# Order edges between weight splits, a later fourth token sum and another tile for two weight pairs, in a float32 decoder layer on one core

## The chip, the cores and the metric

The kernel runs on one core of one Trainium2 chip. The metric is device time in microseconds (us) of one execution, the median over the runs. The core has five engines with a queue each, which they work off in order: TensorE (PE), VectorE (DVE), ScalarE (ACT), GpSimd (POOL) and SyncE (SP), which here only issues DMAs. An engine waits for another one, or for a DMA, by semaphores; what stands behind a waiting instruction on its queue waits with it.

## The reference

One decoder layer with D = 1024, 1024 tokens and a hidden width of 4096, all float32:

```python
z = h @ w_in                       # pool group | q | k | v
y_pool = pool_mixer(u_pool, w_pool, pool_scale)
y_attn = sliding_window_attention(q, k, v, attn_sinks)   # window 128, ALiBi, sinks
mix = concatenate([y_pool, y_attn]) @ w_out
h = layer_norm(DEEPNORM_ALPHA * h + mix, ln1_g, ln1_b)
ff = square(relu(h @ w_ff1)) @ w_ff2
h = layer_norm(DEEPNORM_ALPHA * h + ff, ln2_g, ln2_b)
h = h + sigmoid(h @ w_ple_gate + b_ple_gate) * (p @ w_ple)
```

## The kernel before, in words

**Split products.** A float32 operand is split into a high part, a cast to the reduced type fp32r on ACT (`high`, L98), and a low part, source minus high on DVE (`low`, L103). A product of two split operands is three matmuls (`mm3`): high by high (L112), high by low (L113), low by high (L114). A "product" of the feed-forward layer (`prod`) is four such triples, 12 matmuls of 128x128 by 128x512. It reads one split weight part (tag "ws", six buffers) and one split token matrix in `X` (tag "c", six buffers, or "x7").

**Stages.** First come z, attention and pooling; then the output projection in a left and a right half of columns, for token blocks 0 to 3 and then 4 to 7. `out_left(t, ...)` loads eight weight blocks in four pairs, splits each pair into a "w" tile, of which there are two buffers, and multiplies each by four token blocks; `residual` (L431) adds the sum to the token rows. Layer norm and transposes follow (`norm1`), whose results for blocks 4 to 7 are also combined into the token matrices T1, T2 and T3: with a and b the two transposed halves, T1 = a - (first half of the tokens), T2 = b - T1, T3 = b - a. T4 is made out of T2 by two more adds with X["21"] and a split (`last_sum(c)`, c the token block): three operations on DVE and one on ACT for each of four blocks. While norm1 runs, products a11 and a12 of the first eight weight pairs (NPRE = 8) are made by `early`.

**The first feed-forward matrix.** The main loop (L719 to L735) works a Strassen-Winograd form: a pair p of weight blocks needs the products a11, a12, s2, s3, s1, s4 and a22, seven for p of 8 and above and the last five for p below 8. `source` loads the pair's weights into a "w" tile (four blocks, 1 MB, two buffers) and makes sums of them on DVE: s2 by two adds into a "st" tile, s3 by one add in place, s4 by one more. The order of products is p0: s2, s3, s1, s4; p1: s2, s3, s1, s4; a22 of p0; a22 of p1; then pair after pair. T2 goes with s2, T3 with s3, T1 with s1 and s4 with X["22"]; T4 goes with a22. The loop makes each weight split AHEAD = 4 turns before the product that uses it; in its first four turns it makes only splits, and the T4 sum of one token block each. `finish` adds the products up on DVE and squares the hidden blocks, on ACT mostly; POOL stores them.

**What sets the order.** The source is traced in program order, and the tile framework's scheduler orders each engine's instructions by its own timing model, within the dependences. What the program can add is an edge: instructions traced inside `with tc.issue_after(ins)` stay behind `ins` on its engine. Before, the loop has none.

**After the loop**: the second feed-forward matrix (to about 828 us), the second norm, the gate and the embedding product.

Of the kernel before, what the change touches and what calls it, by code (L numbers as in the profile page):

```python
# [8 lines left out]
F32R = mybir.dt.float32r  # L9
# [3 lines left out]
P = 128  # L13
D = 1024
S = 1024
HALF = 512
# [47 lines left out]
AHEAD = 4  # L64
# [3 lines left out]
def layer(ctx, tc, xT, x, pT, w_in, w_pool, pscale, sinks, w_out, ln1, w1, w2, ln2, w_ple, w_gate, bgate, bias, rcount, out):  # L68
    nc = tc.nc
# [6 lines left out]
    def nm(s):  # L76
        uid[0] += 1
        return f"{s}_{uid[0]}"
# [4 lines left out]
    def wt(shape, dt=F32R):  # L83
        return sb.tile(shape, dt, tag="w", bufs=2, name=nm("w"))

    def nat(shape, dt=F32):
        return sb.tile(shape, dt, tag="n", bufs=8, name=nm("n"))
# [8 lines left out]
    def high(dst, src, scale=None):  # L96
        if scale is None:
            nc.scalar.copy(out=dst, in_=src)  # L98
        else:
            nc.scalar.mul(out=dst, in_=src, mul=scale)  # L100

    def low(eng, dst, src, hi):
        return eng.tensor_tensor(out=dst, in0=src, in1=hi.bitcast(F32), op=ALU.subtract)  # L103
# [60 lines left out]
    def acc_ps():  # L164
        return ps.tile([P, HALF], F32, tag="mm", bufs=3, name=nm("mm"))
# [224 lines left out]
    def layer_norm(y, gb, root=False):  # L390
        st = small([P, 2, 6])
        for i in range(2):
            nc.vector.bn_stats(out=st[:, i, :], in_=y[:, i * HALF : (i + 1) * HALF])
        mv = small([P, 8])
        nc.vector.bn_aggr(out=mv[:, 0:2], in_=st.rearrange("p a b -> p (a b)"))
        v, r0, e, r, m = (mv[:, i : i + 1] for i in range(2, 7))
        nc.vector.tensor_scalar(out=v, in0=mv[:, 1:2], scalar1=LN_EPS, scalar2=None, op0=ALU.add)
        if root:
            nc.vector.reciprocal(out=r0, in_=v)
            nc.scalar.activation(out=r0, in_=r0, func=AF.Sqrt)  # L400
        else:
            nc.gpsimd.tensor_tensor(out=r0, in0=v, in1=mhalf, op=ALU.pow)

        nc.vector.scalar_tensor_tensor(out=e, in0=r0, scalar=v, in1=r0, op0=ALU.mult, op1=ALU.mult)
        nc.vector.tensor_scalar(out=e, in0=e, scalar1=-0.5, scalar2=1.5, op0=ALU.mult, op1=ALU.add)
        nc.vector.tensor_tensor(out=r, in0=r0, in1=e, op=ALU.mult)
        nc.vector.tensor_scalar(out=m, in0=mv[:, 0:1], scalar1=-1.0, scalar2=None, op0=ALU.mult)
        nc.scalar.activation(out=y, in_=y, func=AF.Identity, bias=m, scale=1.0)
        nc.vector.scalar_tensor_tensor(out=y, in0=y, scalar=r, in1=gb[0], op0=ALU.mult, op1=ALU.mult)
        add(y, y, gb[1])  # L410
# [4 lines left out]
    def transposed(y, j, pt):  # L415
        for k in range(4):
            kt = 4 * j + k
            nc.tensor.transpose(pt[:, k, :], y[:, kt * P : (kt + 1) * P], ident)  # L418
        return pt

    def out_load(dst, dh, kk, st, eng):
        load_split(dst[:, 0], dst[:, 1], w_out[dh, kk], None, eng, st)

    def out_mm(o, n, k, w):
        m = (mixP if k < 4 else mixA)[n // 4]
        c = (n % 4) * P
        mm3(o, m[:, 0, k % 4, c : c + P], m[:, 1, k % 4, c : c + P], w[:, 0, k % 2, :], w[:, 1, k % 2, :], k == 0, k == NK - 1)
# [3 lines left out]
        nc.vector.scalar_tensor_tensor(out=v, in0=v, scalar=ALPHA, in1=o, op0=ALU.mult, op1=ALU.add)  # L431


    def out_left(t, staging, eng):
        blocks = range(4 * t, 4 * t + 4)
        os = [acc_ps() for _ in range(3)]
        os.append(ps.tile([P, HALF], F32, tag="s", bufs=2, name=nm("s")))
        for k in range(NK):
            if k % 2 == 0:
                w = wt([P, 2, 2, HALF])  # L440
                out_load(w, 0, k // 2, staging(), eng)
            for n in blocks:
                out_mm(os[n % 4], n, k, w)
        return os
# [51 lines left out]
    def wide(tag, shape, dt):  # L496
        return p1.tile(shape, dt, tag=tag, bufs=1, name=nm(tag))


    X = {}  # L500
# [4 lines left out]
    def split_to(name, c, src, eng):  # L505
        cs = slice(c * P, (c + 1) * P)
        dh = X[name][:, 0, :, cs]
        high(dh, src)
        low(eng, X[name][:, 1, :, cs], src, dh)

    def norm1(n):
        t, c = n // 4, n % 4
        layer_norm(hn[n], gb1)
        a = transposed(hn[n], 0, tr_ps())
        b = transposed(hn[n], 1, tr_av())
        nc.scalar.mul(out=hn[n], in_=hn[n], mul=ALPHA)
        nc.scalar.dma_start(out=h_dram[n], in_=hn[n])
        if t == 0:
            if c < 3:
                nc.scalar.copy(out=pre[:, 4 + c].rearrange("p (k t) -> p k t", k=4), in_=a)  # L520
            split_to("11", c, a, nc.vector)
            split_to("21", c, b, nc.vector)
        else:
            r12, t1, t2 = temp((P, 4, P)), temp((P, 4, P)), nat([P, 4, P])
            nc.scalar.copy(out=r12, in_=a)
            if c < 3:
                add(t1, a, pre[:, 4 + c].rearrange("p (k t) -> p k t", k=4), ALU.subtract)
            else:
                for i in range(2):
                    add(t1, t1 if i else a, block("11", i, c), ALU.subtract)  # L530
            add(t2, b, t1, ALU.subtract)
            split_to("22", c, b, nc.vector)
            add(r12, b, r12, ALU.subtract)
            split_to("T1", c, t1, nc.vector)
            split_to("T2", c, t2, nc.vector)
            split_to("T3", c, r12, nc.vector)
            diff[c] = t2


    diff = {}  # L540

    def last_sum(c):
        t2 = diff[c]
        for i in range(2):
            add(t2, block("21", i, c), t2, ALU.add if i else ALU.subtract)
        split_to("T4", c, t2, nc.vector)

    def w_split(src):
        s = part()
        high(s[:, 0], src)  # L550
        low(nc.vector, s[:, 1], src, s[:, 0])
        return s

    def prod(o, s, name, more=False):
# [27 lines left out]
    for j in range(2):  # L582
        w = big([P, 2, 2, 2, HALF])
# [7 lines left out]
        out_right(n)  # L591
    X["11"], X["21"] = (big([P, 2, 4, HALF]) for _ in range(2))
    pre = wide("pre", [P, NPRE, HALF], F32)
    os = out_left(1, lambda: nat([P, 2, HALF]), nc.vector)
    residual_load(1)
    for n in range(4):
        norm1(n)
# [22 lines left out]
    def source(p, name):  # L620
        first = p >= NLAST and name in ("a11", "a12")
        if (p, first) not in raws:
            r = raws[p, first] = wt([P, 2 if first else 4, 4, P], F32)
            nc.sync.dma_start(out=r, in_=w1[p, :, 0:2] if first else w1[p])
        r = raws[p, first]
        if name in BLOCK:
            return r[:, BLOCK[name]]
        if name == "s2":
            sums[p] = stage([P, 2, 4, P])
            add(sums[p][:, 0], r[:, 2], r[:, 3])  # L630
            add(sums[p][:, 1], sums[p][:, 0], r[:, 0], ALU.subtract)
        elif name == "s3":
            add(r[:, 2], r[:, 0], r[:, 2], ALU.subtract)
            return r[:, 2]
        elif name == "s4":
            add(sums[p][:, 1], r[:, 1], sums[p][:, 1], ALU.subtract)
        return sums[p][:, 0 if name == "s1" else 1]
# [29 lines left out]
    def finish(p, name):  # L667
        if name == "a11":
            U[p, 1] = temp()
            nc.scalar.copy(out=U[p, 1], in_=B[p, "A"])  # L670
        elif name == "s2":
            U[p, 2] = temp()
            add(U[p, 2], pre[:, p] if p < NPRE else U[p, 1], B[p, "B"])
        elif name == "s3":
            U[p, 3] = temp()
            add(U[p, 3], U[p, 2], B[p, "Y"])
        elif name == "s1":
            hidden_block(p, 1, 1, square_sum(U[p, 3], B[p, "Z"]))
        elif name == "a12":
            hidden_block(p, 0, 0, lambda dst: relu2(dst, B[p, "A"]))  # L680
        elif name == "a22":
            hidden_block(p, 1, 0, square_sum(U[p, 2], B[p, "Y"]))
        else:
            hidden_block(p, 0, 1, square_sum_v(U[p, 2], B[p, "Z"]))
# [4 lines left out]
    order = []  # L689
# [26 lines left out]
                nc.sync.dma_start(out=second, in_=src)  # L716
                blocks[u].append(second)

    ready, lows = {}, []  # L719
    for i in range(len(order) + AHEAD):  # L720
        if i == order.index((NLAST, "a11")):
            begin = wide("pre", [P, 4, 2, HALF], F32)
            for u in range(4):
                fetch(u)
        if i < len(order):
            ready[i] = w_split(source(*order[i]))
        if i < AHEAD:
            last_sum(i)
            continue
        p, name = order[i - AHEAD]  # L730
        xb, where, more = STEPS[name]
        if not more:
            B[p, where] = bank()
        prod(B[p, where], ready.pop(i - AHEAD), xb, more)
        finish(p, name)  # L735


    hidden = {}
# [80 lines left out]
    for u, (i, q) in enumerate(units):  # L819
        k = QORDER.index(q)  # L820
# [129 lines left out]
```

## Time and profile before

| | us |
| --- | --- |
| runs | 1013.18, 1011.62, 1015.57; median 1013.18 |
| the profiled execution's own time | 1010.05 |
| its span on the engines | 1008.1 |
| PE busy | 989.4 (98%) |
| DVE, ACT, POOL busy | 704.4, 457.2, 129.1 |

A timeline row gives start, duration, engine, source line, operation with output and inputs, count, and in square brackets how long the engine had been idle and what ended that. Names are the program's tags; "mm", "f" and "s" are accumulators in PSUM, "pt" and "av" transposes in PSUM, "c" and "x" split token matrices, "ws" a split weight part, "w" a weight tile, "st" a staging tile, "n" and "t" token or hidden blocks. Durations overlap at their ends: 128x512 matmuls in a row start 0.227 us apart though each is listed with 0.39. A row of the waits view gives the engine, what it was about to do, what it waited for, and us in total, times and the longest in us. The loop's first product stands at 315.82, and the second matrix begins at about 575.

### The profile page before, as it was taken

How to read it: one execution, taken by the hardware profiler on the slowest of the kernel's cores; microseconds unless marked ns; L12 is line 12 of the kernel's file. 1: busy time of each engine (PE TensorE's matmuls, PEld its weight loads, DVE VectorE, ACT ScalarE, POOL GpSimd, SP SyncE). 2: the span in 40 equal slices, each digit the busy share in tenths (PEclk: the TensorE clock that was granted, in tenths of full speed). 3: DMA queues.
4: the chain of work that ended last, by engine and by line, in shares of the span. 5: the costliest groups of instructions: out<-in, count | busy, mean ns of one | idle time of the engine just before them, and what ended most of it. 6: DMA issues, size and time to landing. Idle time of an engine off the chain costs nothing.

```text
span 1008.1 us, 12163 instructions
## 1 busy us (share of the span) xinstructions
PE 989.4 (98%) x4556; PEld 820.5 (81%) x4556; DVE 704.4 (70%) x1119; ACT 457.2 (45%) x735; POOL 129.1 (13%) x158
## 2 busy tenths in 40 slices
PE   8999999999999999899999999999999999999998
PEld 7877887887887888788888888888888888888887
DVE  5789679566888757655456666787647699997333
ACT  5667567524475433343444343433433354651111
POOL 0034265620000000100000000100011110000000
PEclk9999999999999999999999999999999999999999
DMA  6511423324152533664174793776798874621011
GB/s 214 179 62 46 164 63 126 125 84 146 64 189 105 188 96 106 225 179 146 63 249 168 278 320 132 167 239 200 209 211 186 202 174 125 202 81 42 37 38 42
DMA packets 38715, 148.00 MB, mean 147 GB/s; under 512 B 4736, under 2 KB 5632, under 8 KB 35840
## 3 DMA queue, kind: packets, MB, share of 16 engines
q1 hardware_dynamic: 29664, 116.29, 34.3%
q0 software_dynamic: 7840, 26.74, 11.3%
q10 hardware_dynamic: 1152, 4.19, 1.0%
q8 instruction: 35, 0.57, 0.2%
q14 instruction: 24, 0.20, 0.1%
HBM read 124.66 MB, written 22.54 MB: 146 GB/s over the span
## 4 chain that ended last, share of the span: by engine, by line
PE 59%; DVE 2%; DMA 1%; ACT 0%; issue 0%; DVEq 0%; ACTq 0%
PE f L114 19%; PE f L113 19%; PE f L112 19%; DMA w<-in_w 1%; PE f L418 1%; DVE ws L103 1%; DVE st L117 0%; DVE n L117 0%; DVE t L117 0%; DVE w L117 0%; ACT ws L98 0%; DVE n L663 0%; DVE t L892 0%; DVE t L890 0%; DVE t L893 0%; ACT t L891 0%
## 5 line engine op out<-in xcount | busy, mean ns | idle before, releaser
L114 PE MATMUL f<-c,ws 128*128 128x512 f32 (+1 forms) x456 | 174.6, 386 | 3.2 <-DVE ws L103 3.2
L112 PE MATMUL f<-c,ws 128*128 128x512 f32 (+1 forms) x456 | 175.3, 386 | 1.5 <-ACT c L98 1.5
L113 PE MATMUL f<-c,ws 128*128 128x512 f32 (+1 forms) x456 | 175.7, 385 | 0.0
L113 PE MATMUL f<-x,w 128*128 128x512 f32 x448 | 174.3, 389 | 0.0
L114 PE MATMUL f<-x,w 128*128 128x512 f32 x448 | 174.3, 389 | 0.0
L112 PE MATMUL f<-x,w 128*128 128x512 f32 x448 | 147.1, 389 | 0.0
L98 ACT CAST w<-st 128x1024 fp32r<-128x1024 f32 (+2 forms) x67 | 67.0, 999 | 111.6 <-issue 68.7
L103 DVE TENSOR_TENSOR w<-st,w 128x1024 fp32r<-128x1024 f32 (+2 forms) x63 | 74.2, 1180 | 49.5 <-ACT w L98 49.2
L114 PEld LDWEIGHTS f<-c,ws 128*128 128x128 f32 x456 | 85.7, 188 | 20.9 <-DVE ws L103 3.8
L112 PEld LDWEIGHTS f<-c,ws 128*128 128x128 f32 x456 | 85.6, 188 | 19.0 <-ACT c L98 1.9
L113 PEld LDWEIGHTS f<-c,ws 128*128 128x128 f32 x456 | 85.7, 188 | 17.1
L114 PEld LDWEIGHTS f<-x,w 128*128 128x128 f32 x448 | 84.1, 188 | 17.6
L113 PEld LDWEIGHTS f<-x,w 128*128 128x128 f32 x448 | 84.0, 188 | 17.5
L112 PEld LDWEIGHTS f<-x,w 128*128 128x128 f32 x448 | 84.1, 188 | 17.3
L103 DVE TENSOR_TENSOR x<-ws,x 128x1024 fp32r<-128x1024 f32 x52 | 63.3, 1218 | 0.0
L112 PE MATMUL mm<-c,w 128*128 128x512 f32 x152 | 60.8, 405 | 1.9 <-ACT w L98 1.2
L98 ACT CAST ws<-w 128x512 fp32r<-128x512 f32 x60 | 37.1, 622 | 52.3 <-PE f L114 42.7
L114 PE MATMUL mm<-c,w 128*128 128x512 f32 x152 | 60.4, 401 | 0.0
L113 PE MATMUL mm<-c,w 128*128 128x512 f32 x152 | 60.2, 397 | 0.0
L98 ACT CAST ws<-st 128x512 fp32r<-128x512 f32 x48 | 29.7, 620 | 62.5 <-PE f L114 52.9
L98 ACT CAST x<-ws 128x1024 fp32r<-128x1024 f32 x52 | 54.5, 1049 | 0.0
L117 DVE TENSOR_TENSOR n<-t,f 128x512 f32<-128x512 f32 x48 | 32.0, 682 | 31.4 <-PE f L114 31.4
(200 smaller groups left out, 1815.9 us busy)
## 6 DMA issues: line engine op xcount, KB each, us to landing
ws<-in_w SPq DMA_DIRECT2D x70, 512.0 KB, 4.1
w<-in_w SPq DMA_DIRECT2D x16, 1024.0 KB, 5.3
c<-fd SPq DMA_DIRECT2D x6, 2048.0 KB, 9.0
fd<-n POOLq DMA_DIRECT2D x20, 512.0 KB, 4.1
ws<-in_w POOLq DMA_DIRECT2D x20, 512.0 KB, 7.0
st<-in_w_in SPq DMA_DIRECT2D x18, 512.0 KB, 3.5
w<-in_w SPq DMA_DIRECT2D x10, 512.0 KB, 4.2
n<-in_x SPq DMA_DIRECT2D x8, 512.0 KB, 5.0
```

The lines of the kernel that those rows point to most:

```text
L98: nc.scalar.copy(out=dst, in_=src)
L103: return eng.tensor_tensor(out=dst, in0=src, in1=hi.bitcast(F32), op=ALU.subtract)
L112: nc.tensor.matmul(o, ah, bh, start=first, stop=False, skip_group_check=more)
L113: nc.tensor.matmul(o, ah, bl, start=False, stop=False, skip_group_check=more)
L114: nc.tensor.matmul(o, al, bh, start=False, stop=last, skip_group_check=more)
L117: nc.vector.tensor_tensor(out=o, in0=a, in1=b, op=op)
L418: nc.tensor.transpose(pt[:, k, :], y[:, kt * P : (kt + 1) * P], ident)
```

## The change

Three edits, with no instruction added or removed.

1. In the second `out_left` (blocks 4 to 7) the pairs for k = 4 and k = 6 are split into one tile with the tag "x7" of its own instead of the third and fourth "w" tile. That tag's buffer is later used by X["22"].
2. `w_split` records its low instruction in `lows`, and every weight split of the loop, with the sums that `source` makes for it, is traced behind an edge from the low before it. The first split of the fifth turn has its edge from the low of T3 for the last token block instead. All edges are on DVE, the engine of `low`.
3. `last_sum(c)` moves from the first four turns of the loop to behind the first four products, and behind an edge from the low of T3 for the last token block. For this `split_to` returns its low, and `diff[c]` keeps it.

```diff
-    def out_left(t, staging, eng):
+    def out_left(t, staging, eng, room=None):
...
-                w = wt([P, 2, 2, HALF])
+                w = room[:, k // 2 - 2] if room is not None and k > 3 else wt([P, 2, 2, HALF])
...
-        low(eng, X[name][:, 1, :, cs], src, dh)
+        return low(eng, X[name][:, 1, :, cs], src, dh)
...
-            split_to("T3", c, r12, nc.vector)
-            diff[c] = t2
+            diff[c] = t2, split_to("T3", c, r12, nc.vector)
...
-        t2 = diff[c]
+        t2 = diff[c][0]
...
+    lows = []
+
     def w_split(src):
         s = part()
         high(s[:, 0], src)
-        low(nc.vector, s[:, 1], src, s[:, 0])
+        lows.append(low(nc.vector, s[:, 1], src, s[:, 0]))
         return s
...
-    os = out_left(1, lambda: nat([P, 2, HALF]), nc.vector)
+    os = out_left(1, lambda: nat([P, 2, HALF]), nc.vector, wide("x7", [P, 2, 2, 2, HALF], F32R))
...
-    ready, lows = {}, []
+    ready = {}
     for i in range(len(order) + AHEAD):
...
         if i < len(order):
-            ready[i] = w_split(source(*order[i]))
+            with tc.issue_after((diff[3][1] if i == AHEAD else lows[-1]).ins):
+                ready[i] = w_split(source(*order[i]))
         if i < AHEAD:
-            last_sum(i)
             continue
...
         finish(p, name)
+        if i - AHEAD < 4:
+            with tc.issue_after(diff[3][1].ins):
+                last_sum(i - AHEAD)
```

The scheduler makes the following of it. Names below carry buffer numbers, which are mostly one lower after the change.

DVE in the second `out_left`, before: the lows of the two last weight pairs (w_346, w_348) stand behind a layer norm's last operations (L409, L117).

```order
L405 TENSOR_SCALAR sm_367_2325<-sm_367_2325 128x1
L406 TENSOR_TENSOR sm_367_2325<-sm_367_2325 128x1
L409 SCALAR_TENSOR_TENSOR n_310_1846<-n_310_1846,sm_367_2325,st_329_1990 128x1024
L117 TENSOR_TENSOR n_310_1846<-n_310_1846,st_330_1991 128x1024
L103 TENSOR_TENSOR w_346_2163<-n_347_2164,w_346_2163 128x1024
L103 TENSOR_TENSOR w_348_2192<-n_349_2193,w_348_2192 128x1024
```

After:

```order
L103 TENSOR_TENSOR w_345_2135<-n_346_2136,w_345_2135 128x1024
L316 TENSOR_TENSOR y_286_1733<-av_301_1810,yl_306_1831 64x512
L103 TENSOR_TENSOR x7_338_2101<-n_347_2164,x7_338_2101 128x1024
L103 TENSOR_TENSOR x7_338_2101<-n_348_2192,x7_338_2101 128x1024
L431 SCALAR_TENSOR_TENSOR n_307_1840<-n_307_1840,mm_331_1994 128x512
L103 TENSOR_TENSOR ws_379_2466<-ws_378_2464,ws_379_2466 128x512
```

The two lows (now into x7_338) stand ahead of the first residual add (L431) of the right half for blocks 0 to 3, 47 rows earlier.

DVE at the loop's start, before. c_375 is T1, c_376 T2, c_377 T3 and c_378 T4, t_438 T3's sum, st_454 and w_453 the second pair's weights.

```order
L117 TENSOR_TENSOR st_454_2975<-st_454_2975,w_453_2973 128x512
L117 TENSOR_TENSOR w_453_2973<-w_453_2973 128x512
L103 TENSOR_TENSOR c_378_2464<-n_423_2749,c_378_2464 128x4x128
L117 TENSOR_TENSOR n_440_2866<-av_437_2857,t_439_2865 128x512
L103 TENSOR_TENSOR ws_452_2966<-st_448_2940,ws_452_2966 128x512
L103 TENSOR_TENSOR c_375_2461<-t_439_2865,c_375_2461 128x4x128
L103 TENSOR_TENSOR ws_455_2978<-st_454_2975,ws_455_2978 128x512
L103 TENSOR_TENSOR x7_374_2460<-av_437_2857,x7_374_2460 128x4x128
L117 TENSOR_TENSOR t_438_2864<-av_437_2857,t_438_2864 128x512
L117 TENSOR_TENSOR st_454_2975<-w_453_2973,st_454_2975 128x512
L103 TENSOR_TENSOR c_376_2462<-n_440_2866,c_376_2462 128x4x128
L103 TENSOR_TENSOR ws_458_2997<-w_453_2973,ws_458_2997 128x512
```

After, where c_374 to c_377 are T1 to T4, t_437 T3's sum, and st_453 and w_452 the second pair's weights:

```order
L117 TENSOR_TENSOR n_439_2865<-av_436_2856,t_438_2864 128x512
L103 TENSOR_TENSOR ws_451_2953<-st_447_2939,ws_451_2953 128x512
L103 TENSOR_TENSOR c_374_2460<-t_438_2864,c_374_2460 128x4x128
L103 TENSOR_TENSOR x7_373_2459<-av_436_2856,x7_373_2459 128x4x128
L117 TENSOR_TENSOR t_437_2863<-av_436_2856,t_437_2863 128x512
L103 TENSOR_TENSOR c_375_2461<-n_439_2865,c_375_2461 128x4x128
L103 TENSOR_TENSOR c_376_2462<-t_437_2863,c_376_2462 128x4x128
L117 TENSOR_TENSOR st_453_2958<-w_452_2956 128x512
L117 TENSOR_TENSOR n_388_2514<-c_336_2099,n_388_2514 128x512
L117 TENSOR_TENSOR n_405_2631<-c_336_2099,n_405_2631 128x512
L117 TENSOR_TENSOR n_422_2748<-c_336_2099,n_422_2748 128x512
L117 TENSOR_TENSOR n_439_2865<-c_336_2099,n_439_2865 128x512
```

The lows of T2 and T3 now come ahead of everything of the second pair and of the T4 sums (n_388 to n_439). The T4 sums of all four blocks, eight adds and then four lows, stand in one stretch among the splits of the second pair. On PE the loop now begins with the whole of one product after another (s2 with T2, s3 with T3, s1 with T1); before, it did one matmul of s2 and one of s3, then the whole of s1, and then the rest.

DVE between pairs 7 and 8, before. st_538 and w_537 belong to pair 7, st_556 and w_552 to pair 8.

```order
L117 TENSOR_TENSOR t_536_3589<-pre_337_2100,f_535_3576 128x512
L103 TENSOR_TENSOR ws_534_3573<-w_525_3491,ws_534_3573 128x512
L117 TENSOR_TENSOR st_556_3711<-w_552_3691 128x512
L117 TENSOR_TENSOR st_556_3711<-st_556_3711,w_552_3691 128x512
L117 TENSOR_TENSOR w_552_3691<-w_552_3691 128x512
L117 TENSOR_TENSOR n_519_3450<-t_524_3489,f_531_3518 128x512
L117 TENSOR_TENSOR n_521_3469<-t_524_3489,f_528_3499 128x512
L103 TENSOR_TENSOR ws_539_3596<-st_538_3593,ws_539_3596 128x512
```

After, with st_537 and w_536 of pair 7 and st_555 and w_551 of pair 8:

```order
L103 TENSOR_TENSOR ws_546_3653<-st_537_3592,ws_546_3653 128x512
L103 TENSOR_TENSOR ws_548_3672<-w_536_3590,ws_548_3672 128x512
L117 TENSOR_TENSOR n_545_3649<-t_535_3588,f_542_3617 128x512
L117 TENSOR_TENSOR n_547_3668<-t_535_3588,f_539_3598 128x512
L117 TENSOR_TENSOR t_550_3688<-pre_337_2100,f_549_3675 128x512
L103 TENSOR_TENSOR ws_552_3692<-w_551_3690,ws_552_3692 128x512
L117 TENSOR_TENSOR st_555_3710<-w_551_3690 128x512
L664 SCALAR_TENSOR_TENSOR n_545_3649<-n_545_3649 128x512
```

Pair 8's adds stood ahead of the low of pair 7's first product (ws_539); they now stand behind all five lows of pair 7 (the last is ws_548), and its first split (ws_552) is of a raw block.

On SP two loads of token rows (L449) are now issued one ahead of and one behind the second `early` weight load (L566), where both stood behind it, and four loads for the second matrix (L708) stand together behind a load of pair weights instead of two on each side of it. From about 575 us on, the order is as before.

## The prediction

> **What bounds the kernel now.** I read the page's busy times first, then the windows by stage, then what TensorE waited for. The page:
>
> ```profile
> span 1008.1 us, 12163 instructions
> PE 989.4 (98%) x4556; PEld 820.5 (81%) x4556; DVE 704.4 (70%) x1119; ACT 457.2 (45%) x735; POOL 129.1 (13%) x158
> ```
>
> TensorE (PE) is busy 98% of the span. The change takes no matmul away, so it can gain only PE's idle time. The windows (us of the window, then busy time and count of PE, weight loads, DVE, ACT and POOL; PE's granted clock; DMA share; GB/s) say where that lies:
>
> ```profile
> 200.00:317.70 117.70, 114.58 (x536) 94.31 (x534) 92.43 (x170) 61.12 (x99) 12.83 (x17) 1.00 0.36 126
> 317.70:412.20 94.50, 91.31 (x402) 75.15 (x402) 60.62 (x98) 34.11 (x57) 4.29 (x8) 1.00 0.34 121
> 412.20:575.00 162.80, 162.80 (x718) 134.85 (x719) 95.35 (x148) 71.01 (x121) 10.49 (x17) 1.00 0.53 182
> 575.00:828.00 253.00, 253.00 (x1117) 209.46 (x1117) 183.90 (x192) 101.27 (x107) 22.67 (x26) 1.00 0.76 209
> 828.00:1003.50 175.50, 175.48 (x835) 147.05 (x834) 118.54 (x175) 57.41 (x73) 3.11 (x4) 1.00 0.25 84
> ```
>
> From 412.2 to 1003.5 PE has no gap to give. Before 200 the change alters nothing. What is left is 117.70 - 114.58 = 3.12 and 94.50 - 91.31 = 3.19 us. PE's waits name them:
>
> ```profile
> PE f L114 <- DVE ws L103: 3.2, 1, 3.2
> ...
> PE f L112 <- ACT c L98: 1.5, 1, 1.5
> PE mm L113 <- DVE w L103: 1.4, 1, 1.4
> ...
> PE mm L112 <- DVE n L431: 0.2, 1, 0.2
> ```
>
> Three of the four stand where the change works. A gap costs a little more than the wait, since the matmul after it is followed later than the usual 0.227 us; I count from start to start.
>
> **The change part by part.** The instructions stay the same in number and shape, but for order and buffers.
>
> *Weight pairs in another tile.* In the second half of the output projection PE stops here:
>
> ```profile
> 230.49 0.60 PE L418 MATMUL pt<-ident,n 128*128 128x128 f32 x4
> ...
> 232.62 0.27 PE L418 MATMUL pt<-ident,n 128*128 128x128 f32 x1
> 234.32 0.50 PE L113 MATMUL mm<-w,c 128*128 128x512 f32 x1 [1.44 <-DVE w L103]
> 225.45 0.39 PE L113 MATMUL mm<-w,c 128*128 128x512 f32 x1
> 226.04 0.50 PE L112 MATMUL mm<-w,c 128*128 128x512 f32 x1 [0.20 <-DVE n L431]
> ```
>
> From 232.62 to 234.32 is 1.70 us, of which I leave 0.2 to the transpose itself: the gap is worth 1.5 us. It waits for the low half of a weight pair, which VectorE (DVE) makes at 233.05 because ScalarE (ACT) casts the pair only at 230.38, when a "w" buffer is free:
>
> ```profile
> 230.38 1.98 ACT L98 CAST w<-n 128x1024 fp32r<-128x1024 f32 x2
> 233.05 2.35 DVE L103 TENSOR_TENSOR w<-n,w 128x1024 fp32r<-128x1024 f32 x2
> 210.56 2.33 ACT L98 CAST ws<-ws 128x512 fp32r<-128x512 f32 x4 [7.40 <-DMA ws<-in_w]
> 205.25 0.69 DVE L431 SCALAR_TENSOR_TENSOR n<-n,mm 128x512 f32<-128x512 f32 x1 [2.75 <-PE mm L114]
> 211.22 1.29 DVE L103 TENSOR_TENSOR ws<-ws,ws 128x512 fp32r<-128x512 f32 x2 [4.55 <-ACT ws L98]
> ```
>
> The new tile is free from the start, and the raw pairs have long been loaded. The two casts (1.98) and the two subtractions (2.35) move to about 203 to 207, where ACT idles 7.40 us and DVE 2.75 and 4.55. The residual add at 205.25 slips by about 1.4 us; behind it only norm statistics are queued, before that idle 4.55. PE needs the pair near 230.5, so 23 us cover it: **-1.5 us**. Without that cover the price is at most the old gap. The raw pairs' buffers come free earlier, so one token load passes one weight load on SyncE's (SP) queue; that weight's sums feed products after 255, which leaves room. The other gap in these rows, 226.04 - 225.45 - 0.23 = 0.36 us, waits for a residual add that stays where it is: 0 to -0.36, and I take 0.
>
> *Fourth token sums behind the first products.* At the loop's start PE does one matmul of the T2 product and then waits for T3's last cast:
>
> ```profile
> 315.82 0.39 PE L112 MATMUL f<-c,ws 128*128 128x512 f32 x1
> 317.69 0.73 PE L112 MATMUL f<-c,ws 128*128 128x512 f32 x2 [1.49 <-ACT c L98]
> 317.02 0.62 ACT L98 CAST c<-t 128x512 fp32r<-128x512 f32 x1
> 315.65 0.68 DVE L117 TENSOR_TENSOR t<-av,t 128x512 f32<-128x512 f32 x1
> 316.85 0.69 DVE L103 TENSOR_TENSOR c<-n,c 128x512 fp32r<-128x512 f32 x1
> 318.05 0.69 DVE L103 TENSOR_TENSOR c<-t,c 128x512 fp32r<-128x512 f32 x1
> 323.92 0.69 DVE L117 TENSOR_TENSOR t<-pre,f 128x512 f32<-128x512 f32 x1 [1.60 <-PE f L114]
> ```
>
> T3's sum is made at 315.65 because sums for T4, and three adds on the next pair's weights, stand ahead on DVE. DVE issues one such operation every 0.60 us (316.85 to 318.05 is 1.20 for two). Now nine of the twelve T4 operations that stood ahead of this point, and the three adds, go behind T3. With 0.60 each from the last PSUM transpose I get T2's last low ready at 313.2 and T3's at 314.0; PE arrives, 1.5 earlier than before, at 314.3 and needs T2's low at 314.5 and T3 at 317.1, a whole T2 product (2.72) later. The gap, 317.69 - 315.82 - 0.23 + 0.11, is **-1.75 us**.
>
> What is late next: twelve T4 operations, 12 x 0.60 = 7.2 us on DVE, now stand among the splits of the second pair's weights. By the same count the low half for its T3 product is ready at 325.4 and needed at 326.0. This is the tightest place, 0.6 us. The T4 sums themselves are first read by the ninth product, over 21 us into the loop, so they are in time. Loss from both sides: 0 if the count holds; 1.75 if the wait merely moves here. I take 0.5, nearer to nothing because the count is from measured spacings, but it leaves out DVE's waits on ACT's casts, which from 300 to 425 were (us, times, longest)
>
> ```profile
> DVE ws L103 <- ACT ws L98: 1.6, 5, 0.7
> ```
>
> *Splits in order.* The large stall:
>
> ```profile
> 400.35 0.33 SPq L624 DMA_DIRECT2D w<-in_w  x1
> 408.30 0.69 DVE L117 TENSOR_TENSOR st<-w 128x512 f32<-128x512 f32 x1 [7.98 <-DMA w<-in_w]
> 410.24 1.28 DVE L117 TENSOR_TENSOR n<-t,f 128x512 f32<-128x512 f32 x2
> 411.43 0.68 DVE L103 TENSOR_TENSOR ws<-st,ws 128x512 fp32r<-128x512 f32 x1
> 408.59 0.39 PE L113 MATMUL f<-c,ws 128*128 128x512 f32 x1
> 412.17 0.50 PE L114 MATMUL f<-c,ws 128*128 128x512 f32 x1 [3.19 <-DVE ws L103]
> 412.50 0.39 PE L112 MATMUL f<-c,ws 128*128 128x512 f32 x1
> ```
>
> DVE runs in order. The add at 408.30 belongs to pair 8 and waits for pair 8's weights, whose load went out at 400.35, when their buffer came free. Behind it in the queue stands the low half of pair 7 at 411.43, whose cast was long there, and PE waits for that. With the ordering edges no add of pair 8 precedes a split of pair 7, so this wait goes: 412.17 - 408.59 - 0.23 + 0.11 = **-3.45 us**.
>
> What is queued behind a waiting add now? The edges make each split's sums wait for the previous low, so a late load holds only its own pair's splits and the hidden-layer adds behind them. Each period's weights are still asked for when a buffer comes free. Counting 0.60 per operation and the slowest landing below, I get slacks of 2.8 us or more for every pair from 3 to 8, and 6 or more later. The landing times of the loop's stretch, and the wait ahead of earlier such adds, are:
>
> ```profile
> DMA to landing us min/median/max: 4.6/6.2/7.9
> ```
> ```profile
> 363.09 0.69 DVE L117 TENSOR_TENSOR st<-w 128x512 f32<-128x512 f32 x1 [4.74 <-DMA w<-in_w]
> 378.21 0.69 DVE L117 TENSOR_TENSOR st<-w 128x512 f32<-128x512 f32 x1 [5.93 <-DMA w<-in_w]
> ```
>
> DVE waited on a load in period after period, and PE only once: such a wait costs nothing where the needed low is already made. Bounds for this part: 3.45 gained, or, if the stall was due to the slow landing alone, less by 7.9 - 6.2 = 1.7.
>
> The Trainium skill speaks against this part: "DMA: Bandwidth & Descriptors", section "Anatomy of one DMA — SWDGE (gpsimd) path", fits about 2.0 us plus bytes over 436 GB/s, for these 1 MB an estimated 4.4 us. These loads are issued by SP, not by the path of that fit, and no load in this stretch landed under 4.6 us; by 4.4 the add would start 3.5 us earlier, the stall would not exist, and the sum would lose the whole 3.45. The trace's median of 6.2 lies between.
>
> *Sum.* 1.5 + 1.75 + 3.45 - 0.5 = 6.2 us. The profiled execution took 1010.05 us itself, 1.95 around its span of 1008.1; less 6.2 it is 1003.85. The median of the runs is 1013.18, 3.1 above the profiled one and so with more idle time, of which I credit 0.4 to the same waits: 1013.18 - 6.6 = **1006.6 us**.
>
> **The rivals.**
>
> *A, a late landing.* The stall at 412 is this execution's own, or an equal wait returns at another pair. For it: the load took the longest of its stretch. Against it: DVE waits 5 to 6 us for loads in other periods too, and the order on its queue that lets such a wait through to PE is the same in every run. Gain 1.5 + 1.75, and between none and half of 3.45: 1009.2.
>
> *B, the T4 burst.* The sums late in the loop's first products stall PE at 326 by what was won at 317. For it: 0.6 us of slack against 7.2 us of added work. Against it: DVE idles 1.60 us at 323.92 alone. Gain 1.5 + 3.45 - 0.3: 1008.5.
>
> *C, slower.* The edges chain every split to the one before. If a pair's last low is late, the next pair's adds, which free its raw weights, and so the next load, are late too: then the landing shows once in each of the ten periods from pair 2 to pair 11. From a slip of about 2.8 us (the least slack above) it decides; a period then loses what exceeds that, and with 1.5 us in each of ten periods, against 6.2 won, the time is 1013.18 - 6.2 + 15 = 1022. For it: the landings of 4.6 to 7.9 us and the 8 us wait at 408. Against it: DVE is busy 60.62 of 94.50 us in that stretch, so a slip is made up within a period.
>
> *D, a larger gain.* The runs' 3.1 us above the profiled execution are more of the same waits for loads, and go too: 1013.18 - 6.7 - 3 = 1003.5.
>
> That the change doesn't do what it says I leave out: in the built program the rows stand in the new order.
>
> The Trainium skill, "TensorE: Matmul & The Clock Gate", section "What's actually happening", halves PE's clock after an idle window of about 3.4 us. The 3.35 us gap before 412.17 left the granted clock at 1.00 and the next matmuls 0.23 apart. The rule gives no further gain in this trace; in runs where that gap is longer it would add to D.
>
> **How the numbers follow.** The forecast has 0.57, A 0.18, B 0.11, C 0.05, D 0.09. A measurement of this kernel can tell about 0.5% from no change, here 5.07 us: faster means under 1008.1. The forecast is faster in 0.8 of its cases (its own range is 1004.5 to 1009), D always, B in a third, A in a fifth: 0.46 + 0.09 + 0.04 + 0.03 = 0.62. Slower is C, 0.05; the rest, 0.33, is within 0.5%. The range takes in A and most of D: 1002.8 to 1011.5.
>
> **What would show it.** Right: the three waits of PE on w, c and ws are gone, PE is busy all of 230 to 412 but for a few tenths, and every wait of DVE on w stands behind all lows of the pair before. The lows of the two new pairs start before 207. Wrong: a PE wait on a ws low between 322 and 345 (B), on a ws low at 350 to 420 (A or C; C in period after period), or the wait on the weight pair still at 234. A time of 1010 or more with those waits gone would mean that the time lies outside the trace.

## The result, and the profile after

The changed kernel takes 1003.31 us in the median of its runs (1002.32 to 1004.64), the kernel before beside it 1011.98 (1006.9 to 1015.57, the runs known earlier included). The ratio is 0.9919, with a 95% interval of 0.9891 to 0.9947. Run a second time, beside another set of runs of before (median 1010.31), it took 1003.16, a ratio of 0.9933 [0.991, 0.9957]. The change makes the kernel about 0.7 to 0.8% faster. The forecast was 1006.6, faster.

The page of the profiled execution, whose own time was 1003.32:

```profile
span 1001.4 us, 12182 instructions
PE 988.5 (99%) x4556; PEld 820.1 (82%) x4556; DVE 706.1 (71%) x1119; ACT 459.0 (46%) x735; POOL 129.3 (13%) x158
```

The span is 6.7 us shorter, and TensorE's busy time is the same within 0.9: only idle time went. The same windows as before, cut at the loop's new start:

```profile
200.00:314.20 114.20, 113.72 (x533) 94.04 (x532) 84.73 (x156) 58.23 (x92) 12.94 (x17) 1.00 0.36 128
314.20:405.00 90.80, 90.80 (x403) 75.17 (x402) 71.22 (x114) 39.36 (x65) 5.36 (x10) 1.00 0.39 139
405.00:568.00 163.00, 163.00 (x721) 134.97 (x720) 94.11 (x145) 70.24 (x119) 9.49 (x15) 1.00 0.51 175
```

From 314 to its last matmul near 996.8 TensorE has no gap at all: it is busy all 682.60 us from 314.20 to 996.80. What it still waits for:

```profile
PE mm L112 <- ACT tmp L98: 2.1, 2, 1.7
PE s L283 <- DVE sm L287: 1.5, 2, 1.1
PE pt L378 <- POOL ident masks.py:199: 1.4, 1, 1.4
...
PE mm L112 <- DVE n L431: 0.5, 1, 0.5
PE mm L113 <- DVE c L103: 0.5, 1, 0.5
```

The three waits on a weight pair, on T3's cast and on a weight split's low are gone. The wait for the residual add (L431) is there with 0.5 instead of 0.2, at 221.81. The last row is at 11 us, in a part that the change doesn't touch.

At the three places, DVE's and ACT's rows show the moved work (the two lows and casts of the weight pairs, here named x; the low of the second pair's T3 product; the low of pair 7's first product) beside the matmul that reads it:

```profile
203.11 2.00 ACT L98 CAST x<-n 128x1024 fp32r<-128x1024 f32 x2
204.19 2.60 DVE L103 TENSOR_TENSOR x<-n,x 128x1024 fp32r<-128x1024 f32 x2 [1.64 <-ACT x L98]
206.71 0.68 DVE L431 SCALAR_TENSOR_TENSOR n<-n,mm 128x512 f32<-128x512 f32 x1
...
325.22 0.69 DVE L103 TENSOR_TENSOR ws<-w,ws 128x512 fp32r<-128x512 f32 x1
326.29 0.39 PE L114 MATMUL f<-c,ws 128*128 128x512 f32 x1
...
397.00 0.69 DVE L103 TENSOR_TENSOR ws<-st,ws 128x512 fp32r<-128x512 f32 x1
404.71 0.39 PE L114 MATMUL f<-c,ws 128*128 128x512 f32 x1
```

The pairs are split from 203 to 207, as counted. The low at 325.22 ends at 325.91, 0.4 us before its first use. The low at 397.00 is there 7.0 us early; before, the same low was 3.3 us late. And DVE's waits from 300 to 425 hold no load of w any more, where there were 24.9 us of them:

```profile
DVE ws L103 <- ACT ws L98: 13.5, 7, 4.5
DVE n L117 <- PE f L114: 12.0, 12, 2.1
DVE t L117 <- PE f L114: 2.9, 4, 1.1
```

DVE now waits for ACT and PE, that is, it runs ahead.

### The profile page after: what moved, and what is told of

Read it like the earlier page. It is cut to its first block, busy times and chain, and to the rows that moved or that the text cites. A ratio compares the mean times of both kernels' runs of the same rounds, so it can differ in the third digit from the quotient of the medians.

```text
span 1001.4 us, 12182 instructions
## 1 busy us (share of the span) xinstructions
PE 988.5 (99%) x4556; PEld 820.1 (82%) x4556; DVE 706.1 (71%) x1119; ACT 459.0 (46%) x735; POOL 129.3 (13%) x158
## 4 chain that ended last, share of the span: by engine, by line
PE 91%; DVE 3%; DMA 2%; ACT 2%; issue 1%; POOL 1%; SPq 0%; POOLq 0%; ACTq 0%
PE f L114 22%; PE f L113 22%; PE f L112 22%; PE mm L112 6%; PE mm L113 6%; PE mm L114 6%; DMA ws<-in_w 1%; PE pt L307 1%; PE f L418 1%; DMA st<-in_w_out 1%; PE s L284 1%; PE s L283 1%; DMA n<-in_xT 1%; DVE e L300 0%; ACT e L294 0%
## 5 line engine op out<-in xcount | busy, mean ns | idle before, releaser
L117 DVE TENSOR_TENSOR n<-t,f 128x512 f32<-128x512 f32 x48 | 31.9, 685 | 39.2 <-PE f L114 39.1
L103 DVE TENSOR_TENSOR ws<-w,ws 128x512 fp32r<-128x512 f32 x60 | 41.1, 689 | 24.9 <-ACT ws L98 24.5
```

The lines of the kernel that those rows point to most:

```text
L117: nc.vector.tensor_tensor(out=o, in0=a, in1=b, op=op)
```

## The experiments

All runs of one group stood beside the same runs of the kernel before on the same chip: median 1010.71 (1005.66 to 1016.14) for the first four, 1009.94 (1006.04 to 1015.31) for the second four, 1010.31 (1007.87 to 1011.93) for the last. My theory was that three separate stalls were removed, one by each edit; the rivals were that gains are waited for at the next place, and those of the prediction.

**Without the new tile.**

```diff
-    os = out_left(1, lambda: nat([P, 2, HALF]), nc.vector, wide("x7", [P, 2, 2, 2, HALF], F32R))
+    os = out_left(1, lambda: nat([P, 2, HALF]), nc.vector)
```

> The change without its first edit: the two weight pairs of the second left half go back to the w tiles, everything else as after (DVE and PE orders are those of after). Theory, three separate stalls: the 1.4 us wait for the low of a weight pair near 234 is back and nothing else, so PE idles 1.5 us more than after, span 1001.4 + 1.5 = 1002.9, runs near 1004.8. Rival, what is won at one place is waited for at the next: the loop's start absorbs the 1.5 us, span within 0.5 of 1001.4.

1005.81 us, ratio 0.9946 [0.9923, 0.9969]. (The orders are those of after in the loop; in the output projection itself they are those of before.) The wait is back, and TensorE has none after it:

```profile
235.58 0.50 PE L113 MATMUL mm<-w,c 128*128 128x512 f32 x1 [1.43 <-DVE w L103]
```

The span is 1004.3, 2.9 over that of after, of which this gap is 1.6; 0.5 lies ahead of the change (the last wait before 200 ends at 168.04 instead of 167.51), and 0.4 are small gaps at 221 and 227, the second a longer wait for a residual add. From the loop's start to the last matmul TensorE takes 682.33 us here and 682.03 in after: the loop did not absorb the gap, and the rival falls.

**The new tile alone**, on the kernel before (the second and third edit taken back).

> The first edit alone, on the kernel before (its orders on DVE, ACT and PE are unchanged from before). Theory: the wait near 234 is gone, the waits for T3's cast near 316 (1.5 us) and for the low near 411 (about 3 us, more or less by how long that load takes) stay. Span 1008.1 - 1.5 = 1006.6 if the 411 load takes 7.9 us again, 1.7 less at a landing of 6.2. Rival (the loop's start absorbs it): the wait for T3's cast grows by 1.5 us and the span stays 1008.

1007.58 us, 0.9972 [0.9946, 0.9998]. Again only the orders of the loop are those of before. The wait near 234 is gone, that for T3's cast stays, and that near 411 is shorter with the load:

```profile
316.98 0.74 PE L112 MATMUL f<-c,ws 128*128 128x512 f32 x2 [1.48 <-ACT c L98]
409.46 0.50 PE L114 MATMUL f<-c,ws 128*128 128x512 f32 x1 [1.25 <-DVE ws L103]
```

Its load took 6.89 us instead of 7.86, which is 1.0 of the 1.9 us by which the wait is shorter. The other 1.0 is not the landing: the load went out 9.60 us ahead of the time at which TensorE was ready for the low (398.61 to 408.21), before 8.63 (400.35 to 408.98). In this profile the first edit is worth its own stall, no more.

**The edges alone.**

```diff
         if i < AHEAD:
+            last_sum(i)
             continue
...
-        if i - AHEAD < 4:
-            with tc.issue_after(diff[3][1].ins):
-                last_sum(i - AHEAD)
```

and the weight pairs in w tiles, as in the first experiment.

> Only the edges from split to split, with the T4 sums left in the first four turns and the weight pairs in w tiles. Theory: the wait near 411 goes by the edges alone, the one near 234 stays (1.5 us). The wait for T3's cast: six operations of the second pair's weights leave their place ahead of T3 (3.6 us at 0.60 each), more than the 1.75 us lost there, so it should go by the edges too, although the T4 sums stay; span 1001.4 + 1.5 = 1002.9. Rival, the T4 sums ahead of T3 make that wait: 1.5 us of it stays, span 1004.5.

1005.98 us, 0.9944 [0.9921, 0.9967]. After 200 TensorE waits only once, for the weight pair:

```profile
236.47 0.50 PE L113 MATMUL mm<-w,c 128*128 128x512 f32 x1 [1.44 <-DVE w L103]
```

Both loop waits are gone, T3's too, although the T4 sums stand where they stood. So the T4 sums do not make that wait by themselves: with the second pair's operations gone from ahead of T3, it is gone too. The rival falls. One thing more has changed: TensorE now does the whole product with T2 (12 matmuls) before its first with T3, where before one matmul stood ahead, so that it also asks for T3 later. How much of the 1.75 us each of the two removed was not separated. (The span, 1005.2, is over the expected 1002.9; a stretch at half clock, below, and a late start make up for that.)

**The moved T4 sums alone.**

```diff
-            with tc.issue_after((diff[3][1] if i == AHEAD else lows[-1]).ins):
-                ready[i] = w_split(source(*order[i]))
+            ready[i] = w_split(source(*order[i]))
```

and the weight pairs in w tiles.

> Only the move of the T4 sums behind the loop's first products (each still behind T3's low), no edges between splits, weight pairs in w tiles. Theory: the wait for T3's cast (1.75 us) goes, the waits near 234 (1.5) and near 411 (3.45 in the trace of before, 1.7 at a landing of 6.2) stay, since pair 8's adds still stand ahead of the low of pair 7's first product; span 1006.3, down to 1004.6. Rival, the 411 stall was a late landing of one execution: no wait on a ws low over 0.5 us, span 1003.

1005.23 us, 0.9949 [0.9926, 0.9972]. My expectation failed: the stall near 411 is gone without any edge between splits. Yet the cause is still there, and DVE waits for it as before:

```profile
396.53 0.33 SPq L625 DMA_DIRECT2D w<-in_w  x1
402.57 0.69 DVE L117 TENSOR_TENSOR st<-w 128x512 f32<-128x512 f32 x1 [6.07 <-DMA w<-in_w]
...
405.11 0.68 DVE L103 TENSOR_TENSOR ws<-st,ws 128x512 fp32r<-128x512 f32 x1
```

Pair 8's add still stands ahead of the low of pair 7's first product, and waits 6.07 us for its load. But this load goes out at 396.53 instead of 400.35, and the low ends at 405.8, while the matmul that reads it starts at 406.74: 0.9 us of room. DVE came there earlier because after 350.26 it waits for no other load, where before it did so at 363, 378 and 392: with the T4 sums elsewhere, the scheduler ordered the loop's adds differently. (As in the kernel with the edges alone, a whole product with T2 stands ahead of T3 on TensorE.) The rival, that the stall was one late landing, predicted this outcome from another cause; the second and third profile of before, further down, tell them apart.

**Each load made later.** In three kernels the weights of pairs 2 to 8 are loaded twice into the same tile:

```diff
             nc.sync.dma_start(out=r, in_=w1[p, :, 0:2] if first else w1[p])
+            if 2 <= p <= 8:
+                nc.sync.dma_start(out=r, in_=w1[p])
```

> The kernel before, with the weights of pairs 2 to 8 loaded twice into the same tile, one load after the other, so that they land some 5 us later; orders on PE, DVE and ACT are unchanged, the output too. Theory: before, VectorE works in a ring of landing, sums, splits, free buffer, next load. Its waits for loads end 14.3 us apart on average (350.89 to 408.30 in four steps), more than the 13.6 us that TensorE needs for a pair, and the lag reaches TensorE at 412. With 5 us more in each turn the ring sets the pace for pairs 3 to 8: 25 to 35 us more, 1036 to 1046, with a wait of TensorE in most of these periods. Rival, the stall at 412 was one late landing and the waits otherwise have room: under 6 us more, below 1017.

> The kernel after with the same doubled loads. Theory: the loads go out 9.8 to 16 us ahead of their first use (344.71 to 354.51 is the shortest), two landings take about 11 us, and what is missing is covered by splits that stand 3 us or more ahead: no wait of TensorE, 1003.3 within 1.5 us. Rival C of the prediction, each landing shows once in a period because every split waits for the one before: 1.2 us or more in each of six periods, 1010 or more.

> The kernel after without the edges from split to split (first and third edit kept), with the same doubled loads. Without doubling, the third edit alone had no stall near 411 although VectorE waited 6.07 us for pair 8's load ahead of the low of pair 7's first product. If the edges do nothing that the moved sums don't do already, this equals the after kernel with doubled loads, within 1 us. If they keep late loads away from TensorE, the wait grows to 11 us and TensorE waits 5 us or more there: 1008 or more, and at least 4 us over the after kernel with doubled loads.

Before with doubled loads: 1009.35 us, 1.0007 [0.9984, 1.003]; after: 1007.33, 0.9964 [0.9941, 0.9986]; without edges: 1007.78, 0.9969 [0.9949, 0.999]. The first two expectations failed, and the first of them rests on a statement that is wrong: the orders are not unchanged. (Its rival, under 6 us more, came true, but not in the order that it was about.) Of the third, the branch in which the edges add nothing came true: with and without them the kernels agree within 0.5 us. The scheduler counts the second load and rearranges DVE's queue. In the doubled kernel of before it put pair 8's first add behind the lows of pair 7's first three products; it had stood ahead of all of them. The wait for the low is gone there, although DVE waits 5.68 us for the load:

```profile
412.48 0.69 DVE L117 TENSOR_TENSOR st<-w 128x512 f32<-128x512 f32 x1 [5.68 <-DMA w<-in_w]
...
413.83 0.50 PE L112 MATMUL f<-x,ws 128*128 128x512 f32 x1 [1.13 <-DVE n L117]
```

What is behind the waiting add now is an add on a hidden block, and TensorE waits 1.13 us for the bank that it frees. So this run does not test a late load in a given order; it shows that the order, not the landing alone, made the stall.

The doubled kernel without edges has its longest wait at the same place and of the same kind. DVE waits for loads ten times between 300 and 460, 32.5 us in all, pair 8's add again stands behind the lows of pair 7's first three products, and TensorE waits for the bank:

```profile
412.56 0.50 PE L112 MATMUL f<-x,ws 128*128 128x512 f32 x1 [2.07 <-DVE n L117]
```

The kernel after with doubled loads has one new wait of TensorE, at pair 2, while DVE's waits for loads in the same stretch add up to 3.3 us:

```profile
341.11 0.69 DVE L117 TENSOR_TENSOR st<-w 128x512 f32<-128x512 f32 x1 [1.34 <-DMA w<-in_w]
343.29 0.50 PE L112 MATMUL f<-c,ws 128*128 128x512 f32 x1 [2.49 <-ACT ws L98]
345.05 0.63 PE L112 MATMUL f<-c,ws 128*128 128x512 f32 x1
345.48 0.63 PE L113 MATMUL f<-c,ws 128*128 128x512 f32 x1
```

Pair 2's weights can only be asked for when the first pair's last split has freed the buffer, and doubled they are late; nothing of that kind follows at pairs 3 to 8. That is rival C at one pair and not in every period. And it costs more than its 2.5 us, by the clock (last section).

**A larger T4 burst.** Two more operations per T4 sum, a matrix added and taken away again:

```diff
             add(t2, block("21", i, c), t2, ALU.add if i else ALU.subtract)
+        for i in range(2):
+            add(t2, t2, block("21", 1, c), ALU.subtract if i else ALU.add)
```

> The kernel after with two more operations per T4 sum (a matrix added and taken away again), eight in all, six of them ahead of the low of the second pair's T3 product, behind which the four T4 lows now stand: two operations more than after ahead of that low, 1.2 us. In the trace of after that low ends near 325.9 and TensorE needs it at 326.3, 0.4 us later. Theory, that place is as tight as this: a wait of TensorE on a ws low of 0.6 to 1.0 us near 326, span about 1002.2. If there is more room than that, no wait there.

One run, 1006.07 us. The wait is there and as large as said:

```profile
327.50 0.69 DVE L103 TENSOR_TENSOR ws<-w,ws 128x512 fp32r<-128x512 f32 x1
328.24 0.50 PE L114 MATMUL f<-c,ws 128*128 128x512 f32 x1 [0.72 <-DVE ws L103]
```

The place is tight, by two operations of 0.60: the prediction's rival B lacked 0.4 us of coming true. (The rest of the time lies ahead of the loop, a stretch at half clock near 168 above all.)

**The tile and the T4 sums, without edges, beside after itself.**

> The change without its second edit: weight pairs in the x7 tile and T4 sums behind the first products, no edges between splits. The runs with one edit each showed that the moved T4 sums alone and the edges alone had neither the wait for T3's cast nor the one near 411. Theory now, either of the two is enough: equal to the after kernel within 1 us in the mean, ratio of the two within 0.2%, no wait of TensorE over 0.7 us after 200. Rival, the edges are needed in most executions, because VectorE still waits 6 us for pair 8's load ahead of a needed low: 2 to 4 us slower than after.

> The kernel after, unchanged, beside the kernel without edges on the same chip: 1003.3 within 1 us, no wait of TensorE over 0.7 us after 200 in the profile.

1003.31 us (1002.29 to 1005.3), 0.9939 [0.992, 0.9959], against 1003.16 (1002.56 to 1003.69), 0.9933 [0.991, 0.9957]: the same within what can be measured. Either the edges or the moved sums suffice to keep the loop free of waits, the edges by the third experiment, which was without the tile. But without edges DVE still waits 5.97 us for pair 8's load, and the low behind it (402.54, ending at 403.2) is read at 404.27:

```profile
400.00 0.69 DVE L117 TENSOR_TENSOR st<-w 128x512 f32<-128x512 f32 x1 [5.97 <-DMA w<-in_w]
...
402.54 0.68 DVE L103 TENSOR_TENSOR ws<-st,ws 128x512 fp32r<-128x512 f32 x1
```

That is 1.0 us of room, where the kernel with edges has 7.0. That two of the five runs without edges, at 1005.16 and 1005.3, come from landings over a us longer would fit, but was not shown. Their mean granted clock is 0.997, that of the other three 0.999, and a stretch at half clock (last section) would explain that as well.

**Two more profiles of the kernel before.**

> The kernel before, unchanged, for a second profile. If its runs differ by how late pair 8's load lands (rival D of the prediction), the waits near 234 (1.44 us) and 316 (1.49 us) repeat to 0.1 us, and the one near 411 differs from 3.19 by about as much as the landing differs from 7.86 us. If the spread of the runs lies elsewhere, the wait near 411 repeats within 0.5 us while the span differs by 2 us or more.

> The same for a third profile of the kernel before: the wait near 411 follows the landing of pair 8's load; where it passes about 2.5 us the granted clock may fall behind it, as after the 2.49 us wait of the kernel with doubled loads, for 1.6 us more.

They took 1012.79 and 1006.62 us, with spans of 1011.0 and 1004.8. The second profile, with the load's entry in the chain of waits:

```profile
317.38 0.74 PE L112 MATMUL f<-c,ws 128*128 128x512 f32 x2 [1.58 <-ACT c L98]
382.01 0.50 PE L114 MATMUL f<-c,ws 128*128 128x512 f32 x1 [0.60 <-DVE ws L103]
413.74 0.79 PE L114 MATMUL f<-c,ws 128*128 128x512 f32 x1 [4.24 <-DVE ws L103]
414.33 0.63 PE L112 MATMUL f<-c,ws 128*128 128x512 f32 x1
```

```profile
400.78 8.99 DMA w<-in_w
```

and the third:

```profile
316.96 0.73 PE L112 MATMUL f<-c,ws 128*128 128x512 f32 x2 [1.49 <-ACT c L98]
408.88 0.50 PE L114 MATMUL f<-c,ws 128*128 128x512 f32 x1 [0.73 <-DVE ws L103]
```

```profile
399.18 5.74 DMA w<-in_w
```

With the first profile and the tile alone, whose loop has the same order, this makes four executions:

| landing of pair 8's load, us | from its issue to TensorE being ready for the low, us | TensorE's wait near 411, us | span, us |
| --- | --- | --- | --- |
| 5.74 | 8.97 | 0.73 | 1004.8 |
| 6.89 | 9.60 | 1.25 | 1005.8 (without the 1.5 near 234, with about 1.4 at half clock near 168) |
| 7.86 | 8.63 | 3.19 | 1008.1 |
| 8.99 | 8.72 | 4.24 | 1011.0 |

In all four the wait is the landing plus 3.96 us less the second column, within 0.01. The 3.96 us are DVE's six operations from the landed load to the end of the low, 0.60 each, and small delays. Over the whole range 3.25 us more of landing give 3.5 us more of wait, and the span grows with the wait: from the third profile to the first 2.5 of 3.3 us are this wait, from the third to the second 3.5 of 6.2. T3's wait repeats within 0.1. The one near 234 does not quite: 1.00 to 1.44. The stall at 411 is a property of the order, its size one of the execution.

## Why the prediction was right, and where it was off

**What bounds the kernel**: right. TensorE's busy time did not move, and the gain is idle time of the stretch from 200 to 412.

**The tile, -1.5**: right, with its own stall removed alone and brought back alone. I gave the gap that I left at 226 a bound of 0.36 gained and nothing lost. It is absent in the profiles of after's second run and of the kernel without edges, within that bound, but 0.64 us in the first profile of after, outside it.

**The T4 sums, -1.75, and the edges, -3.45**: the two gaps went, with the sizes given, but the attribution failed. Each edit alone removes both gaps in the profiled executions. For the first gap I blamed the T4 sums and counted only three adds of the second pair with them; the edges take six of that pair's operations, 3.6 us, from ahead of T3, more than the gap. For the second I took the order of the loop as given where no edge changes it; but moving T4 made the scheduler rearrange it too, and the waits for loads at pairs 5 to 7, which made pair 8's load late, went with that. That both gaps went although I had the two edits' shares wrong is luck in the sum: the two together remove what each removes alone. The edges with the new tile, but without the moved sums, were not run.

**The burst, +0.5**: nothing in the profile, with 0.4 us of room against the 0.6 counted; the enlarged burst confirms the place and the price of rival B. I also had T4 first read by the ninth product, over 21 us into the loop; in the built order it is the eighth, 19.0 us into it. The last T4 low ends at 325.3 and the first read is at 333.5, so nothing hung on it.

**The sum**: 6.2 us from 1010.05 gave 1003.85 for the profiled execution, and the profiled execution of after took 1003.32, about the 0.5 for the burst less. The step that was mis-sized comes after it: "of which I credit 0.4 to the same waits". The median known then lay 3.1 us above the profile, and I carried 2.7 of that over to the changed kernel. So the measured 1003.3 lies outside the forecast's own 1004.5 to 1009, in the part of the range that was there for rival D.

After, the runs lie within 2.3 us, and their median is the profiled one; the excess is gone. In good part it was the same wait. The profiled executions of before differ by 6.2 us in span as pair 8's load lands 5.74 to 8.99 us after its issue, and of these 6.2 us the wait near 411 is 3.5, half clock right behind it about 1.4, and a shorter wait for a low at 382 another 0.6. Rival D, to which I gave 0.09, named it, and its 1003.5 is what was measured. That all of the excess was waits for loads is not shown, since most runs have no profile. Their granted clock goes with their length: of the 64 runs of before that stand beside the experiments, the 26 with a mean clock of 0.999 or 1.000 have a median span of 1006.0 us, the 13 with 0.996 or less one of 1012.4. Late loads and half clock were not separated there.

The dependence on the load could have been read from the profile before: the page says that the wait was for a load, the landings spread from 4.6 to 7.9, and a stall that ends on the slowest of them can be expected to differ from run to run. The median of before also came down, to 1009.9 to 1010.7 in the larger sets of runs, so that the gain itself, about 7 to 8.7 us, is nearer to the 6.6 forecast than the time is.

**Rival A** named the late landing for the size of the stall, and this is shown; but not for its being there. At 5.74, under the 6.2 of the median landing, TensorE still waits 0.73. A landing of 4.4 us, the estimate for 1 MB by the fit of the Trainium skill ("DMA: Bandwidth & Descriptors", section "Anatomy of one DMA — SWDGE (gpsimd) path"), would have taken the whole wait away; no landing of this load was near it. **Rival B** missed by 0.4 us. **Rival C** did not occur: no wait of DVE for a load stands in the way of TensorE in the profiles of after, and with doubled loads it showed at one pair only, not in each.

What stays open: how much the edges are worth in the executions with the latest loads. A late load in a fixed order was not measured, since every edit that delays the load also made the scheduler reorder the kernel. With doubled loads, each kernel in an order of its own, the edges gave nothing that can be measured (1007.33 with, 1007.78 without).

## What to carry to other kernels

On an in-order engine, an instruction that waits for a transfer should not stand ahead of one whose inputs are there and whose result is needed; an edge that pins this order gives room (7.0 us instead of 1.0 in the profiles here), even where another edit already happens to remove the stall. Where a stall ends on a DMA, read its size as a spread over executions, and allow for the runs' excess over the profile going with it. A scheduler that works from modelled times can move far-off instructions with a small edit, as it did here with the T4 sums and the doubled loads, so compare the orders over the whole program before putting a gain down to one edit.

## What the runs showed of the hardware that was not expected

**The clock can fall after a gap of 2.5 us, and need not after 3.35.** In the kernel after with doubled loads, eight 128x512 matmuls from 345.05 on stood 0.43 us apart instead of 0.23, 1.6 us lost behind a wait of 2.49. After the wait of 4.24 us in the second profile of before the granted clock was 0.50, and about 1.4 us were lost:

```profile
413.74:416.00 2.26, 2.26 (x5) 1.81 (x6) 2.26 (x4) 0.64 (x2) 1.06 (x2) 0.50 0.04 18
```

In the first profile the gap of 3.35 us ahead of 412.17 was followed by full speed. A fall was also seen in three of the fourteen profiles in a part that no edit touches: after waits of 0.8, 1.1 and 0.4 us between 161 and 168, here in the kernel with the tile alone:

```profile
167.60:171.20 3.60, 3.60 (x10) 2.77 (x10) 3.57 (x6) 2.28 (x9) 1.08 (x1) 0.53 0.82 273
```

In all five profiles with such a stretch it lasts 3.41 us (345.03 to 348.44 in the kernel after with doubled loads), and it starts a whole number of such steps after the clock first rose. So the steps run freely, and a gap can fall across two of them. The gap of 3.35 us did: TensorE was busy 61% of one step and 46% of the next. How busy a step must be is not settled here: the clock fell behind steps with TensorE busy 0, 51 and 55 to 56%, but not behind this one with 46%.

The Trainium skill, "TensorE: Matmul & The Clock Gate", section "What's actually happening", puts the fall after an idle window of about 3.4 us that runs freely, and full speed after a busy one. The steps agree with that, and a window that runs freely would explain that the same waits slow the clock in one execution and not in the next. That a window has to be idle throughout does not agree with the 2.49 us measured here: in the step ahead of 345.03 TensorE was busy for 1.7 us. Such a stretch costs 1.4 to 1.6 us, beside the 2.3 us by which the runs of the kernel after differ at all.
